# First weight group of a fused GLA/RetNet trunk: tokens loaded on a second queue, larger pieces, ScalarE splits, pinned order

## Chip, cores and metric

The kernel runs on one core of one Trainium2 chip. The metric is the device time of one execution in microseconds (us). Three runs of the kernel before took 1416.07, 1416.16 and 1417.53 us; their median, 1416.16 us, is the time before.

## What is computed

Two layers on 256 tokens of width 2048, each with a residual add, and a final RMSNorm. Layer one is gated linear attention, layer two is retention. Cut to what matters here:

```
h = x
h = h + gla_mixer(rms_norm(h, gla_norm), w_in, w_a1, w_a2, b_a, head_g, w_out)
    proj  = h @ w_in                       # q, k, v, gate
    log_a = log_sigmoid((h @ w_a1) @ w_a2 + b_a) / 16     # low-rank decay, rank 16
    o     = chunked attention with decay; o = rms(o) * head_g
    return (o * silu(gate)) @ w_out
h = h + retention_mixer(rms_norm(h, ret_norm), ...)
return rms_norm(h, final_norm)
```

All data are float32. The kernel keeps float32 accuracy by splitting each operand into two float32r parts: `hi`, the operand rounded by a copy, and `lo`, the operand minus `hi`. A product is then hi·hi + hi·lo + lo·hi.

## The kernel before

All weights lie in 60 groups of 2048 x 512 (16 k-tiles of 128 rows, called kt here). A group is loaded in four `raw` tiles of four k-tiles (1 MB, SyncE's queue, SP). Each raw tile is split in two halves of two k-tiles ("a pair"): ScalarE (ACT) writes `hi` (L151) and VectorE (DVE) writes `lo` (L152). TensorE (PE) then multiplies. Three buffers each of raw, hi and lo let the splits run ahead of TensorE.

The change is in the first group, `gqk0` (q and k of GLA head 0), which `group_w` computes: for each pair `j` = 0..7 and each k-tile, four matmuls of weight-hi with both parts of the tokens (L219, 512 columns) and four of weight-lo with the tokens' hi (L220, 256 columns), into four PSUM tiles. While it runs, the tokens have to be prepared too: `x_t`, the transposed input, comes in tiles `xt0`..`xt3` of four k-tiles (L281), and `make_xhl(kt)` writes the two parts of one k-tile of tokens times the norm's weight `gla_norm` (in `smalls`, L292) to `xhl`: the hi part by a TENSOR_SCALAR (L287) and the lo part by a SCALAR_TENSOR_TENSOR (L288), both on VectorE. In program order `make_xhl` for the k-tiles of pair j+1 is called in `first_group(j)`.

`first_group` also computes the low-rank decay's first product `zps` = x_t · w_a1 (L369, 48 columns of weights, 512 of tokens, one matmul a k-tile). For it `w_a1` is loaded (L309, `wa1_src`) and split by ScalarE (L345) and VectorE (L346) into `wa1`. In program order the two `zps` matmuls of pair j-1 stand behind the gqk matmuls of pair j. A memset of `wa2_src` on GpSimd (POOL, L355), which takes over the buffer of `xt0`, and the loads of `w_a2` (L357) and of `mask_t` (L353, a table first used in the attention scores) follow at j = 6.

The order on each engine isn't the program's: a scheduler of the tile layer orders the instructions by a timeline that it reckons at build time. What is wrapped in `keep` (`tc.keep_in_program_order`) stays in its place in program order; in the kernel before no gqk matmul is. `tc.stamp_issue_order_token(ins, "first")`, new in the change, fixes the order of the stamped instructions among each other. On the chip each engine, and each DMA queue, goes through its list strictly in order, held up only by semaphores.

Before the first weights come, two f32 matmuls on zeros (L272) run on TensorE, and ScalarE's first ACTIVATE (L266), on `lnone`, brings the load of its function table ahead of the first split.

Of the kernel before, what the change touches and what calls it, by code (L numbers as in the profile page):

```python
# [10 lines left out]
F32 = mybir.dt.float32  # L11
# [3 lines left out]
AF = mybir.ActivationFunctionType  # L15
ALU = mybir.AluOpType

P = 128
# [5 lines left out]
SUB = 2  # L24
# [31 lines left out]
def kernel(  # L56
# [17 lines left out]
    nc = tc.nc  # L74
# [17 lines left out]
    mm = nc.tensor.matmul  # L92
    keep = tc.keep_in_program_order
# [12 lines left out]
    def emit_raw(parts=1):  # L106
        c = emitted["raw"]
        if c >= n_groups * raws_per_group:
            return
        t = raw_p.tile([P, CHUNK, GW], F32, tag="raw", name=f"raw{c}")  # L110
        g, j = divmod(c, raws_per_group)
        src = w_all[g, :, j * CHUNK * GW : (j + 1) * CHUNK * GW].rearrange("p (k n) -> p k n", n=GW)
        step = CHUNK // parts
        raws[c] = t
        emitted["raw"] += 1

        def load(k):
            nc.sync.dma_start(t[:, k * step : (k + 1) * step, :], src[:, k * step : (k + 1) * step, :])

        if parts > 1:  # L120
            return load
        load(0)
# [13 lines left out]

    tails = []

    def emit_split(pieces=1):
        i = emitted["sub"]  # L140
        if i >= n_groups * NSUB:
            return
        c, j = divmod(i, per_raw)
        while emitted["raw"] <= min(c + DMA_LOOK, n_groups * raws_per_group - 1):
            emit_raw()
        src = raws[c][:, j * SUB : (j + 1) * SUB, :]
        hi, lo = split_tiles(i)
        step = SUB // pieces
        for k in range(pieces):
            sl = slice(k * step, (k + 1) * step)  # L150
            nc.scalar.activation(hi[:, sl], src[:, sl], AF.Copy)  # L151
            nc.vector.tensor_tensor(lo[:, sl], src[:, sl], hi[:, sl].bitcast(F32), ALU.subtract)  # L152
        splits[i] = (hi, lo)
        if j == per_raw - 1:
            del raws[c]
        emitted["sub"] += 1
# [46 lines left out]
    def group_w(rhs, name, extra=None):  # L203
        ps = [acc_p.tile([P, 2, SEQ], F32, tag="acc", name=f"{name}_ps{c}") for c in range(4)]
        for j in range(NSUB):
            hi, lo = next_weights()
            last = j == NSUB - 1
            order = [(q, c) for q in range(SUB) for c in range(4)]
            if last:
                order = [(q, c) for c in range(4) for q in range(SUB)]  # L210
            for q, c in order:
                kt = j * SUB + q
                wh = hi[:, q, c * P : (c + 1) * P]
                wl = lo[:, q, c * P : (c + 1) * P]
                if kt == NKT - 1:
                    mm(ps[c][:, 0, :], wl, rhs[:, kt, 0, :], start=False, stop=False)
                    mm(ps[c], wh, rhs[:, kt, :, :], start=False, stop=True)
                else:
                    mm(ps[c], wh, rhs[:, kt, :, :], start=kt == 0, stop=False)  # L219
                    mm(ps[c][:, 0, :], wl, rhs[:, kt, 0, :], start=False, stop=False)  # L220
            if extra is not None:
                extra(j)
            advance()
        return ps
# [38 lines left out]

    lnone = const([P, 2], "lnone")
    nc.gpsimd.memset(lnone, 1.0)
    nc.scalar.activation(lnone[:, 1:2], lnone[:, 0:1], AF.Copy)  # L266
    lnone = lnone[:, 0:1]
    warm = sg_p.tile([P, GW], F32, tag="sg", name="warm")
    nc.gpsimd.memset(warm, 0.0)
    warm_ps = mis_p.tile([P, GW], F32, tag="mis", name="warm_ps")  # L270
    for _ in range(2):
        mm(warm_ps, warm[:, 0:P], warm, start=True, stop=True)  # L272

    xts = {}

    def load_xt(c):
        t = t4_p.tile([P, 4, SEQ], F32, tag="t4", name=f"xt{c}")
        xts[c] = t

        def load(lo, hi):  # L280
            nc.sync.dma_start(t[:, lo:hi, :], x_t[:, c * 4 + lo : c * 4 + hi, :])  # L281

        return load

    def make_xhl(kt):
        src, g = xts[kt // 4][:, kt % 4, :], sm[:, S_GN + kt : S_GN + kt + 1]
        nc.vector.tensor_scalar(xhl[:, kt, 0], src, g, None, ALU.mult)  # L287
        nc.vector.scalar_tensor_tensor(  # L288
            xhl[:, kt, 1], src, g, xhl[:, kt, 0].bitcast(F32), ALU.mult, ALU.subtract
        )  # L290

    nc.scalar.dma_start(sm, smalls)  # L292
    x0 = load_xt(0)
    x0(0, 1)
    w0 = emit_raw(4)
    w0(0)
    x0(1, 2)
    w0(1)
    x0(2, 4)
    w0(2)  # L300
    w0(3)
    x1 = load_xt(1)
    x1(0, 2)
    w1 = emit_raw(2)
    w1(0)
    x1(2, 4)
    w1(1)
    wa1_src = t4_p.tile([P, NKT, 16], F32, tag="qk", name="wa1_src", bufs=1)
    nc.sync.dma_start(wa1_src, w_a1)  # L309
    load_xt(2)(0, 4)  # L310
    emit_raw()
    make_xhl(0)
    emit_split(2)
    make_xhl(1)
    wa1 = t4_p.tile([P, NKT, 48], F32R, tag="lc", name="wa1", bufs=1)
    nc.gpsimd.memset(wa1.bitcast(F32), 0.0)

# [25 lines left out]
    def first_group(j):  # L343
        if j == 0:
            nc.scalar.activation(wa1[:, :, 0:16], wa1_src, AF.Copy)  # L345
            nc.vector.tensor_tensor(  # L346
                wa1[:, :, 32:48], wa1_src, wa1[:, :, 0:16].bitcast(F32), ALU.subtract
            )
        if j == 1:
            load_xt(3)(0, 4)  # L350
        if j == 6:
            keep(nc.sync.dma_start(ident, ident_in))
            nc.sync.dma_start(mask_t, mask_in)  # L353
            wr = t4_p.tile([80, 2, GW], F32, tag="t4", name="wa2_src")
            nc.gpsimd.memset(wr, 0.0)  # L355
# [12 lines left out]
        for kt in kts if j else ():  # L368
            mm(zps, wa1[:, kt, :], xhl[:, kt, :, :], start=kt == 0, stop=kt == NKT - 1)  # L369
# [622 lines left out]
```

## Time and profile before

| what | value |
|---|---|
| median of 3 runs | 1416.16 us |
| the profiled execution's own time | 1417.53 us |
| its span in the profile | 1415.8 us |
| TensorE busy | 1403.9 us, 99% of the span |
| VectorE, ScalarE, GpSimd busy | 908.6, 690.4, 46.1 us |
| first gqk matmul, first matmul of the next group (gv) | 4.70, 36.14 us |
| HBM read | 263.49 MB |

The profile lists, for each engine, how long it was busy, and for each idle stretch what ended it (the releaser). In the timeline a row is one or several equal instructions: start, length, engine, line, operation, output<-inputs, shape, count, and in brackets the idle time ahead of it and its releaser. The view by windows gives for a stretch of time the busy time of each engine, then the clock that TensorE was granted (1.00 is full) and the DMA engines' share and rate. Times count from the start of the span. The profiled execution is the slowest of the three; it took 1.7 us more than its span.

### The profile page before, as it was taken

What the parts mean: (1) busy time and instruction counts of PE and PEld (TensorE: products, weight loads), DVE (VectorE), ACT (ScalarE), POOL (GpSimd) and SP (SyncE); (2) the same over time, 40 slices, a digit from 0 to 9 for tenths busy, and PEclk for the clock granted to TensorE, in tenths of its full rate; (3) what the DMA queues carried; (4) which work ended last, traced back from release to release, by engine and by line L of the source; (5) the groups of instructions that cost most, each with busy time, mean ns of one, the idle gap of its engine ahead of it and who ended that gap; (6) DMA issues with size and microseconds to landing.
All of it is one profiled execution on the core that took longest, in us unless ns stands there. A gap on an engine that the chain in (4) does not pass through costs nothing.

```text
span 1415.8 us, 17504 instructions
## 1 busy us (share of the span) xinstructions
PE 1403.9 (99%) x6800; PEld 1180.0 (83%) x6800; DVE 908.6 (64%) x1430; ACT 690.4 (49%) x889; POOL 46.1 (3%) x98
## 2 busy tenths in 40 slices
PE   8999999999999999999999999999999999999997
PEld 6888888888888888888888888888888888888887
DVE  6685796545845774665766666665556666666664
ACT  3665655534555655554444444444334444444453
POOL 0001020000010020000000000000000000000000
PEclk9999999999999999999999999999999999999999
DMA  8654555555555555555555555555555555555662
GB/s 287 240 177 149 192 180 175 183 204 180 177 179 178 188 189 179 178 178 183 190 194 192 194 189 198 179 199 181 203 182 184 196 184 199 182 203 176 209 212 94
DMA packets 40499, 266.72 MB, mean 188 GB/s; under 512 B 4880, under 2 KB 5392, under 8 KB 9696
## 3 DMA queue, kind: packets, MB, share of 16 engines
q1 hardware_dynamic: 37536, 257.57, 53.9%
q0 software_dynamic: 2160, 6.95, 1.5%
q8 instruction: 53, 0.87, 0.2%
q10 hardware_dynamic: 720, 1.09, 0.2%
q14 instruction: 30, 0.25, 0.0%
HBM read 263.49 MB, written 2.10 MB: 188 GB/s over the span
## 4 chain that ended last, share of the span: by engine, by line
PE 99%; DMA 0%; SPq 0%; DVE 0%; ACT 0%; issue 0%
PE rqk_ps L219 8%; PE gv_ps L184 4%; PE gg_ps L185 4%; PE rv_ps L184 4%; PE gv_ps L185 4%; PE gv_ps L186 4%; PE rv_ps L185 4%; PE rv_ps L186 4%; PE gg_ps L186 4%; PE gg_ps L184 4%; PE rg_ps L184 4%; PE rg_ps L185 4%; PE rg_ps L186 4%; PE rqk_ps L220 4%; PE gqk_ps L219 4%; PE gb_ps L184 2%
## 5 line engine op out<-in xcount | busy, mean ns | idle before, releaser
L152 DVE TENSOR_TENSOR lo<-raw,hi 128x1024 fp32r<-128x1024 f32 (+1 forms) x473 | 576.6, 1222 | 420.7 <-ACT hi L151 419.9
L151 ACT ACTIVATE hi<-raw 128x1024 fp32r<-128x1024 f32 (+1 forms) x473 | 499.5, 1057 | 614.4 <-PE rg_ps L186 104.6
L219 PE MATMUL rqk_ps<-xhl,hi 128*128 128x512 f32 x480 | 166.9, 398 | 0.0
L220 PE MATMUL rqk_ps<-xhl,lo 128*128 128x256 f32 x480 | 126.4, 280 | 0.0
L219 PEld LDWEIGHTS rqk_ps<-xhl,hi 128*128 128x128 f32 x480 | 88.8, 188 | 17.5
L185 PE MATMUL gg_ps<-lo,xhl 128*128 128x512 f32 x256 | 100.5, 393 | 0.0
L185 PE MATMUL gv_ps<-lo,xhl 128*128 128x512 f32 x256 | 100.4, 392 | 0.0
L185 PE MATMUL rv_ps<-lo,xhl 128*128 128x512 f32 x256 | 100.4, 392 | 0.0
L186 PE MATMUL gv_ps<-hi,xhl 128*128 128x512 f32 x256 | 100.3, 392 | 0.0
L186 PE MATMUL gg_ps<-hi,xhl 128*128 128x512 f32 x256 | 100.0, 391 | 0.0
L186 PE MATMUL rv_ps<-hi,xhl 128*128 128x512 f32 x256 | 99.7, 389 | 0.0
L185 PE MATMUL rg_ps<-lo,xhl 128*128 128x512 f32 x256 | 99.6, 389 | 0.0
L186 PE MATMUL rg_ps<-hi,xhl 128*128 128x512 f32 x256 | 99.6, 389 | 0.0
L184 PE MATMUL gv_ps<-hi,xhl 128*128 128x512 f32 x256 | 93.1, 391 | 0.0
L184 PE MATMUL rv_ps<-hi,xhl 128*128 128x512 f32 x256 | 92.1, 390 | 0.0
L220 PEld LDWEIGHTS rqk_ps<-xhl,lo 128*128 128x128 f32 x480 | 89.1, 189 | 3.4
L184 PE MATMUL rg_ps<-hi,xhl 128*128 128x512 f32 x256 | 91.8, 389 | 0.0
L184 PE MATMUL gg_ps<-hi,xhl 128*128 128x512 f32 x256 | 91.8, 391 | 0.0
L219 PE MATMUL gqk_ps<-xhl,hi 128*128 128x512 f32 x240 | 81.2, 406 | 1.6 <-ACT hi L151 1.6
L220 PE MATMUL gqk_ps<-xhl,lo 128*128 128x256 f32 x240 | 57.9, 283 | 0.5 <-DVE lo L152 0.5
L186 PEld LDWEIGHTS rv_ps<-hi,xhl 128*128 128x128 f32 x256 | 48.1, 188 | 10.0
L186 PEld LDWEIGHTS rg_ps<-hi,xhl 128*128 128x128 f32 x256 | 48.0, 188 | 10.0
(265 smaller groups left out, 2381.8 us busy)
## 6 DMA issues: line engine op xcount, KB each, us to landing
raw<-in_w_all SPq DMA_DIRECT2D x238, 1024.0 KB, 4.9
resid<-in_x_n SPq DMA_DIRECT2D x2, 1024.0 KB, 8.0
gg<-in_gn_g POOLq DMA_DIRECT2D x8, 256.0 KB, 3.8
gb<-in_gn_b POOLq DMA_DIRECT2D x8, 256.0 KB, 4.5
dm<-in_dmat POOLq DMA_DIRECT2D x8, 192.0 KB, 2.6
raw<-in_w_all SPq DMA_DIRECT2D x4, 256.0 KB, 5.0
raw<-in_w_all SPq DMA_DIRECT2D x2, 512.0 KB, 7.4
xt<-in_x_t SPq DMA_DIRECT2D x2, 512.0 KB, 8.5
```

What stands on the lines that cost most here:

```text
L151: nc.scalar.activation(hi[:, sl], src[:, sl], AF.Copy)
L152: nc.vector.tensor_tensor(lo[:, sl], src[:, sl], hi[:, sl].bitcast(F32), ALU.subtract)
L184: mm(ps, xh, hi[:, q, :], start=kt == 0, stop=False)
L185: mm(ps, xh, lo[:, q, :], start=False, stop=False)
L186: mm(ps, xl, hi[:, q, :], start=False, stop=kt == NKT - 1)
L219: mm(ps[c], wh, rhs[:, kt, :, :], start=kt == 0, stop=False)
L220: mm(ps[c][:, 0, :], wl, rhs[:, kt, 0, :], start=False, stop=False)
```

## The change

Seven edits, all in the start of the kernel:

- The tokens of k-tiles 0 and 1 are loaded by ScalarE's DMA queue, the first of them ahead of `smalls`; ScalarE's table load follows these three issues.
- Larger pieces: the second half of `raw0` comes in one DMA in place of two, `xt1` in one in place of two; `w_a1` is loaded behind `xt2`, no longer ahead of it.
- The hi part of the tokens of k-tiles 1 to 7 is made by ScalarE in place of VectorE.
- One of the two warming matmuls is cut to 128 columns.
- The first splits and the first four k-tiles of tokens are stamped to stay in program order, and `make_xhl(1)` is called between the two pieces of the first split.
- For pairs 0 to 2 of the first group all gqk matmuls are kept in program order, four hi and then four lo for each k-tile.
- The mask's load goes from SyncE's to GpSimd's queue, later in program order.

```diff
-        def load(k):
-            nc.sync.dma_start(t[:, k * step : (k + 1) * step, :], src[:, k * step : (k + 1) * step, :])
+        def load(k, n=1):
+            sl = slice(k * step, (k + n) * step)
+            nc.sync.dma_start(t[:, sl, :], src[:, sl, :])
...
-            nc.scalar.activation(hi[:, sl], src[:, sl], AF.Copy)
-            nc.vector.tensor_tensor(lo[:, sl], src[:, sl], hi[:, sl].bitcast(F32), ALU.subtract)
+            a = nc.scalar.activation(hi[:, sl], src[:, sl], AF.Copy)
+            b = nc.vector.tensor_tensor(lo[:, sl], src[:, sl], hi[:, sl].bitcast(F32), ALU.subtract)
+            if i == 0:
+                first(a, b)
+                if k == 0:
+                    between()
...
+            if j < 3 and extra is not None:
+                for q in range(SUB):
+                    kt = j * SUB + q
+                    for c in range(4):
+                        keep(mm(ps[c], hi[:, q, c * P : (c + 1) * P], rhs[:, kt, :, :], start=kt == 0, stop=False))
+                    for c in range(4):
+                        keep(mm(ps[c][:, 0, :], lo[:, q, c * P : (c + 1) * P], rhs[:, kt, 0, :], start=False, stop=False))
+                order = []
...
-    for _ in range(2):
-        mm(warm_ps, warm[:, 0:P], warm, start=True, stop=True)
+    mm(warm_ps, warm[:, 0:P], warm, start=True, stop=True)
+    mm(warm_ps[:, 0:P], warm[:, 0:P], warm[:, 0:P], start=True, stop=True)
...
+    def first(*ins):
+        for x in ins:
+            tc.stamp_issue_order_token(x.ins, "first")
...
-        nc.vector.tensor_scalar(xhl[:, kt, 0], src, g, None, ALU.mult)
-        nc.vector.scalar_tensor_tensor(
+        if 0 < kt < 8:
+            a = nc.scalar.activation(xhl[:, kt, 0], src, AF.Copy, scale=g)
+        else:
+            a = nc.vector.tensor_scalar(xhl[:, kt, 0], src, g, None, ALU.mult)
+        b = nc.vector.scalar_tensor_tensor(
...
+    x0 = load_xt(0)
+    x0(0, 1, nc.scalar)
     nc.scalar.dma_start(sm, smalls)
-    x0 = load_xt(0)
-    x0(0, 1)
+    x0(1, 2, nc.scalar)
+    nc.scalar.activation(lnone2, lnone, AF.Copy)
     w0 = emit_raw(4)
     w0(0)
-    x0(1, 2)
     w0(1)
     x0(2, 4)
-    w0(2)
-    w0(3)
-    x1 = load_xt(1)
-    x1(0, 2)
+    w0(2, 2)
+    load_xt(1)(0, 4)
     w1 = emit_raw(2)
     w1(0)
-    x1(2, 4)
     w1(1)
     wa1_src = t4_p.tile([P, NKT, 16], F32, tag="qk", name="wa1_src", bufs=1)
+    load_xt(2)(0, 4)
     nc.sync.dma_start(wa1_src, w_a1)
-    load_xt(2)(0, 4)
     emit_raw()
     make_xhl(0)
-    emit_split(2)
-    make_xhl(1)
+    emit_split(2, lambda: make_xhl(1))
...
-            nc.sync.dma_start(mask_t, mask_in)
...
+        nc.gpsimd.dma_start(mask_t, mask_in)
```

How this moves the lists of instructions, at the places that the prediction speaks of. TensorE before, at the first use of `wa1`: `hi3` and `lo3` are the parts of pair 3, `hi4` of pair 4, `gqk0_ps` are the group's four PSUM tiles; a row's bracket names the semaphore it waits for.

```order
L219 MATMUL gqk0_ps2_162<-xhl_100,hi3_196 128x512
L220 MATMUL gqk0_ps2_162<-xhl_100,lo3_197 128x256
L219 MATMUL gqk0_ps3_163<-xhl_100,hi3_196 128x512
L220 MATMUL gqk0_ps3_163<-xhl_100,lo3_197 128x256
L369 MATMUL zps_159<-xhl_100,wa1_151 48x512 [waits DVE_49]
L369 MATMUL zps_159<-xhl_100,wa1_151 48x512 x7
L369 MATMUL zps_159<-xhl_100,wa1_151 48x512 [waits DVE_49] x4
L219 MATMUL gqk0_ps0_160<-xhl_100,hi4_226 128x512 [waits Activation_49]
```

TensorE in the changed kernel, at the first use of `wa1` (its lines have higher numbers: L152 and L153 are the splits L151 and L152, L220 and L222 the gqk matmuls, L306 and L307 the tokens' L287 and L288, L386 is `zps`).

```order
L222 MATMUL gqk0_ps2_160<-xhl_100,lo1_163 128x256
L222 MATMUL gqk0_ps3_161<-xhl_100,lo1_163 128x256
L386 MATMUL zps_157<-xhl_100,wa1_149 48x512 [waits DVE_49]
L386 MATMUL zps_157<-xhl_100,wa1_149 48x512
L220 MATMUL gqk0_ps0_158<-xhl_100,hi2_168 128x512
L220 MATMUL gqk0_ps1_159<-xhl_100,hi2_168 128x512
```

Before, the scheduler put the first twelve `zps` matmuls behind pair 3; now the first two stand behind pair 1, the kept matmuls of pair 2 come after them, and two more follow each later pair.

VectorE in the changed kernel, from the split of pair 1 to the one of pair 4.

```order
L153 TENSOR_TENSOR lo1_163<-raw0_123,hi1_162 128x1024 [waits DMAHW6_49,Activation_49]
L307 SCALAR_TENSOR_TENSOR xhl_100<-xt1_128,smalls_97,xhl_100 128x256 [waits DMAHW7_49,Activation_49]
L307 SCALAR_TENSOR_TENSOR xhl_100<-xt1_128,smalls_97,xhl_100 128x256 [waits Activation_49] x3
L153 TENSOR_TENSOR lo2_169<-raw1_130,hi2_168 128x1024 [waits DMAHW0_49,Activation_49]
L153 TENSOR_TENSOR lo3_195<-raw1_130,hi3_194 128x1024 [waits DMAHW1_49,PE_49,Activation_49]
L306 TENSOR_SCALAR xhl_100<-xt2_134,smalls_97 128x256 [waits DMAHW2_49]
L306 TENSOR_SCALAR xhl_100<-xt2_134,smalls_97 128x256 x3
L364 TENSOR_TENSOR wa1_149<-wa1_src_133,wa1_149 128x16x16 [waits DMAHW3_49,Activation_49]
L307 SCALAR_TENSOR_TENSOR xhl_100<-xt2_134,smalls_97,xhl_100 128x256 [waits DVE_49] x4
```

The lo part of `wa1` (L364), for which the first `zps` matmul waits, stands behind `lo3` and four TENSOR_SCALAR of `xt2`; before it stood behind `lo3` too, ahead of the tokens of `xt2`.

SyncE's queue in the changed kernel, from its first DMA.

```order
L119 DMA raw0_123<-in_w_all 128x512 x2
L293 DMA xt0_118<-in_x_t 128x512
L119 DMA raw0_123<-in_w_all 128x1024
L293 DMA xt1_128<-in_x_t 128x1024
L119 DMA raw1_130<-in_w_all 128x1024 [waits DMAHW0_49]
L119 DMA raw1_130<-in_w_all 128x1024 [waits DMAHW1_49]
L293 DMA xt2_134<-in_x_t 128x1024 [waits DMAHW2_49]
L329 DMA wa1_src_133<-in_w_a1 128x256 [waits DMAHW3_49]
L119 DMA raw2_137<-in_w_all 128x2048 [waits DMAHW4_49]
```

Before, this list began with the tokens of k-tile 0, the tokens of k-tile 1 stood between the first two pieces of `raw0`, and `wa1_src` stood between `raw1` and `xt2`. GpSimd's list has one row more: the mask's DMA, directly behind the memset of `wa2_src`. Behind the first GLA head the lists agree row for row.

More of the change, by code (lines that the diff above doesn't have):

```diff
@@ L137, with emit_split @@
     tails = []
-    def emit_split(pieces=1):
+    def emit_split(pieces=1, between=None):
         i = emitted["sub"]
@@ L265 @@
     nc.gpsimd.memset(lnone, 1.0)
-    nc.scalar.activation(lnone[:, 1:2], lnone[:, 0:1], AF.Copy)
-    lnone = lnone[:, 0:1]
+    lnone, lnone2 = lnone[:, 0:1], lnone[:, 1:2]
     warm = sg_p.tile([P, GW], F32, tag="sg", name="warm")
@@ L278, in load_xt, with load @@
         xts[c] = t
-        def load(lo, hi):
-            nc.sync.dma_start(t[:, lo:hi, :], x_t[:, c * 4 + lo : c * 4 + hi, :])
-        return load
+        def load(lo, hi, eng=nc.sync):
+            eng.dma_start(t[:, lo:hi, :], x_t[:, c * 4 + lo : c * 4 + hi, :])
+        return load
+    def first(*ins):
+        for x in ins:
+            tc.stamp_issue_order_token(x.ins, "first")
     def make_xhl(kt):
         src, g = xts[kt // 4][:, kt % 4, :], sm[:, S_GN + kt : S_GN + kt + 1]
-        nc.vector.tensor_scalar(xhl[:, kt, 0], src, g, None, ALU.mult)
-        nc.vector.scalar_tensor_tensor(
+        if 0 < kt < 8:
[3 more added lines that the diff above has]
+        b = nc.vector.scalar_tensor_tensor(
             xhl[:, kt, 1], src, g, xhl[:, kt, 0].bitcast(F32), ALU.mult, ALU.subtract
         )
+        if kt < 4:
+            first(a, b)
+    x0 = load_xt(0)
+    x0(0, 1, nc.scalar)
     nc.scalar.dma_start(sm, smalls)
-    x0 = load_xt(0)
-    x0(0, 1)
+    x0(1, 2, nc.scalar)
+    nc.scalar.activation(lnone2, lnone, AF.Copy)
     w0 = emit_raw(4)
     w0(0)
-    x0(1, 2)
     w0(1)
     x0(2, 4)
-    w0(2)
-    w0(3)
-    x1 = load_xt(1)
-    x1(0, 2)
+    w0(2, 2)
+    load_xt(1)(0, 4)
     w1 = emit_raw(2)
     w1(0)
-    x1(2, 4)
     w1(1)
     wa1_src = t4_p.tile([P, NKT, 16], F32, tag="qk", name="wa1_src", bufs=1)
+    load_xt(2)(0, 4)
     nc.sync.dma_start(wa1_src, w_a1)
-    load_xt(2)(0, 4)
     emit_raw()
     make_xhl(0)
-    emit_split(2)
-    make_xhl(1)
+    emit_split(2, lambda: make_xhl(1))
     wa1 = t4_p.tile([P, NKT, 48], F32R, tag="lc", name="wa1", bufs=1)
```

## Prediction

> **What bounds the kernel now.** I read the page's engine table first, then the list of waits of TensorE alone, then TensorE's timeline up to the first matmul of the second group.
>
> ```profile
> span 1415.8 us, 17504 instructions
> PE 1403.9 (99%) x6800; PEld 1180.0 (83%) x6800; DVE 908.6 (64%) x1430; ACT 690.4 (49%) x889; POOL 46.1 (3%) x98
> ...
> PE warm_ps L272 <- POOL warm L269: 1.8, 1, 1.8
> PE gqk_ps L219 <- ACT hi L151: 1.6, 2, 1.2
> PE gqk_ps L220 <- DVE lo L152: 0.5, 1, 0.5
> ```
>
> TensorE is busy for 99% of the span, and the whole list of its waits has three lines, all in the first 13 us. So the change can take nothing off the rest of the kernel; it can shift the moment at which the first group is done, and everything behind moves by as much. The first group in TensorE's timeline:
>
> ```profile
> 4.70 1.96 PE L219 MATMUL gqk_ps<-xhl,hi 128*128 128x512 f32 x4
> ...
> 7.50 1.19 PE L219 MATMUL gqk_ps<-xhl,hi 128*128 128x512 f32 x4 [0.36 <-ACT hi L151]
> ...
> 10.35 1.19 PE L219 MATMUL gqk_ps<-xhl,hi 128*128 128x512 f32 x4 [1.20 <-ACT hi L151]
> 12.09 0.83 PE L220 MATMUL gqk_ps<-xhl,lo 128*128 128x256 f32 x4 [0.55 <-DVE lo L152]
> ...
> 15.28 1.43 PE L219 MATMUL gqk_ps<-xhl,hi 128*128 128x512 f32 x4
> ...
> 21.23 2.94 PE L369 MATMUL zps<-xhl,wa 128*48 128x512 f32 x12
> 24.02 1.08 PE L219 MATMUL gqk_ps<-xhl,hi 128*128 128x512 f32 x4
> ...
> 26.82 1.09 PE L219 MATMUL gqk_ps<-xhl,hi 128*128 128x512 f32 x4
> ...
> 36.14 0.47 PE L184 MATMUL gv_ps<-hi,xhl 128*128 128x512 f32 x1
> ```
>
> K-tile 0 starts at 4.70, k-tile 1 at 7.50, pair 1 (k-tiles 2 and 3) at 10.35, pair 2 at 15.28, and the next group at 36.14. From 12.09 on TensorE never waits. A pair takes 2.80 us at full clock (24.02 to 26.82). The clock is the second thing to see, in stretches chosen to fit its changes:
>
> ```profile
> core 0: us, PE busy (x) PEld busy (x) DVE busy (x) ACT busy (x) POOL busy (x), PEclk, DMA share, GB/s
> 2.00:9.00 7.00, 6.63 (x20) 3.88 (x20) 3.71 (x9) 1.92 (x4) 0.94 (x5) 1.00 0.87 264
> 10.00:13.00 3.00, 2.10 (x9) 1.59 (x10) 2.72 (x6) 1.36 (x2) 0.49 (x1) 0.93 1.03 411
> 9.18:12.59 3.41, 1.69 (x8) 1.18 (x9) 2.61 (x6) 2.11 (x2) 0.95 (x1) 1.00 1.02 403
> 12.59:16.00 3.41, 3.41 (x13) 2.93 (x12) 3.41 (x7) 1.36 (x2) 0.00 (x0) 0.50 1.04 430
> 16.00:19.40 3.40, 3.40 (x20) 2.88 (x20) 3.40 (x11) 1.89 (x2) 0.00 (x0) 1.00 1.10 370
> ```
>
> In the 3.41 us from 9.18 TensorE was busy for 1.69, half the time; in the next 3.41 us it was granted half the clock, and, busy throughout, full clock after that. The price was 3.41 x 0.5 = 1.7 us of work. So the idle times of 1.20 and 0.55 us cost themselves and 1.7 us more.
>
> Everything from pair 2 on needs 36.14 - 15.28 = 20.86 us, of which 0.36 is the half clock's (0.72 us, 15.28 to 16.00, at half speed): **20.50 us of work**, six pairs and all sixteen `zps`. The change leaves this work as it is. So the result follows from two numbers: when TensorE is let through to pair 2 and its first `zps`, against 15.28, and how much half clock comes after, against 0.36.
>
> **The change, part by part.** The part that decides is not named in the change's title. The first two `zps` now stand behind pair 1 and ahead of the kept matmuls of pair 2. They wait for the lo part of `wa1`, and TensorE goes in order: pairs 2 to 7, all of the 20.50 us, queue behind that wait. Before, the same `zps` stood behind pair 3 and waited for nothing (21.23 has no bracket). On VectorE the lo part of `wa1` stands behind `lo3` and four TENSOR_SCALAR of `xt2`; `lo3` needs `hi3`, and `hi3` the second half of `raw1`. So TensorE now waits for data of pair 3 before it may start pair 2. The chain's durations:
>
> ```profile
> 9.24 1.06 ACT L151 ACTIVATE hi<-raw 128x1024 fp32r<-128x1024 f32 x1 [1.80 <-DMA raw<-in_w_all]
> ...
> 13.51 1.06 ACT L151 ACTIVATE hi<-raw 128x1024 fp32r<-128x1024 f32 x1 [0.97 <-DMA raw<-in_w_all]
> 14.47 0.40 ACT L345 ACTIVATE wa<-wa_src 128x256 fp32r<-128x256 f32 x1
> ...
> 15.20 1.21 DVE L152 TENSOR_TENSOR lo<-raw,hi 128x1024 fp32r<-128x1024 f32 x1
> 16.33 0.41 DVE L346 TENSOR_TENSOR wa<-wa_src,wa 128x256 fp32r<-128x256 f32 x1
> 16.67 1.13 DVE L287 TENSOR_SCALAR xhl<-xt,smalls 128x256 fp32r<-128x256 f32 x4
> 17.72 0.47 DVE L288 SCALAR_TENSOR_TENSOR xhl<-xt,smalls,xhl 128x256 fp32r<-128x256 f32 x1
> ```
>
> `hi3` takes 1.06 us, `lo3` 1.13 (15.20 to 16.33, the next start), the four TENSOR_SCALAR 1.05 (16.67 to 17.72), the lo part of `wa1` 0.41; with 0.1 for the hand-overs, an estimate, 3.75 us from the arrival of `raw1`'s second half.
>
> That arrival was 13.51 before. Three edits move it. The order of the bytes ahead is the same, but 0.786 MB of them (`raw0`'s second half, half of `xt1`) come in rows of 4 KB in place of 2 KB. The stretch with the small pieces, 2 to 9 us, ran at 264 GB/s, the one with mostly 4 KB rows at 411: 0.786 MB take 1.91 in place of 2.98 us, a gain of 1.07. I take all of it, since nothing else in the two rows differs as clearly; the other end is no gain. The tokens on ScalarE's queue let the first weights be issued at 0.74 in place of 1.19:
>
> ```profile
> 0.74 0.39 SPq L281 DMA_DIRECT2D xt<-in_x_t  x1
> 1.19 0.42 SPq L118 DMA_DIRECT2D raw<-in_w_all  x1
> ...
> 10.27 0.33 SPq L353 DMA_DIRECT2D mask<-in_mask  x1
> ...
> 9.54 0.95 POOL L355 MEMSET wa_src<- 80x1024 f32 x1 [6.60 <-DVE xhl L288]
> ```
>
> That is between 0 and 0.45 us for the bytes behind, and I take 0.22. The mask, issued at 10.27 behind everything of the first pairs before, now follows GpSimd's memset, which began at 9.54 when the tokens of k-tile 3 were done and would begin about 1 us earlier; its 0.26 MB (0.64 us at 411 GB/s) run on another queue beside `raw1` and may delay it by 0 to 0.64; I take 0.32. The mask itself isn't waited for before the attention scores. So `raw1`'s second half arrives at 13.51 - 1.07 - 0.22 + 0.32 = 12.54, and the first `zps` starts at **16.29**. `w_a1` and `xt2`, next in the queue, carry 0.66 MB, 1.6 us: there by 14.1, and ScalarE's 0.40 is done by 14.6, before VectorE is through `lo3` (14.8). Bounds: all 3.18 MB ahead at 411 GB/s from 2.0 us give 9.7, and `zps` at 13.5; no gain at all and the mask's full price give 14.15, and `zps` at 17.9. I stay near the row of before.
>
> TensorE is through with pair 1 well ahead of that. `raw0`'s second half arrived at 9.24; less 0.71 (0.524 MB at the better rate) and 0.22 that is 8.31; `hi1` 1.06 and `lo1` 1.21 end at 10.6, and the last twelve matmuls of the pair, two thirds of 2.80 us, at 12.5. It then **idles for 3.8 us**, as long as the stretch after which the clock was halved, which had been idle for 1.7 us only. So I count another stretch at half clock, 1.7 us, all of it now on the 20.50 us. Released half-way it is 0.85; if the stretch in which work resumes doesn't count and a second follows, 3.4.
>
> The sum: 16.29 - 15.28 = +1.01 for the wait, 1.70 - 0.36 = +1.34 for the clock: **+2.35 us**. The other edits come out at nothing. The three removed waits (0.36, 1.20, 0.55) and the 1.35 us of half clock ahead of 15.28 all lie before the new wait, which swallows any gain. The seven TENSOR_SCALAR taken from VectorE (1.13 a four) and put on ScalarE (0.40 each, by the row of the same shape) lie there too, since ScalarE was waiting for loads in both rows above. The shorter warming ends sooner, but k-tile 0 waits for its split anyway; at worst the clock rises one stretch later, which is again ahead of the wait. Were the wait hidden, that cover would be gone, and the removed idle times would count in full.
>
> A rule of the Trainium skill speaks against the gain in loading: the page "DMA: Bandwidth & Descriptors", section "🎯 Rules for kernel authors", says that spreading DMAs over several engines brings no bandwidth, only the sequencers' issue time. By it the 0.22 may stand, and the second queue gives nothing else; the sum would not change by more.
>
> **From the span to the time.** The profiled execution took 1417.53 us for its span of 1415.8; with the change it would take 1419.88. It was the slowest of the three; on their median, 1416.16, the forecast is **1418.5 us**. The wait between 15.6 and 17.0 and a price of 1.3 to 2.3 us for the clock give 1417.4 to 1419.8.
>
> **Rivals.**
>
> - *The loads come no sooner.* For it: the 264 GB/s may be those of a queue that is just starting, not of short rows. Arrival 13.51 - 0.22 + 0.64 = 13.93, `zps` at 17.68, +2.40 + 1.34 = +3.74: 1419.9; with two stretches of half clock 1421.6.
> - *The clock holds through the stall.* Against it: the row 9.18:12.59, where 1.7 us of idle time sufficed. For it: one case only. Then +1.01 - 0.36 = +0.65: 1416.8. The page "TensorE: Matmul & The Clock Gate" of the Trainium skill, section "🎯 Why this matters for your kernels", allows gaps up to about 3 us and takes the clock back after a whole idle window; by that rule the gaps of before, 1.20 and 0.55, would have been free, which the trace contradicts.
> - *Faster: the loads run at full pace from the first byte.* Arrival 9.7, `zps` at 13.45: -1.83 + 1.34 = -0.49, 1415.7; with the clock held too, 1414.0. It turns at `raw1`'s second half arriving before 10.2. Against it: k-tiles 0 and 1 still come in the 1 and 2 KB rows of the 264 GB/s stretch.
> - *The change doesn't do what it says*: TensorE doesn't stop at the first `zps`, since VectorE has `wa1` by 12.5. For that `raw1` would have to be there at 8.8, before the earliest bound; I give it nothing of its own.
>
> **How the numbers follow.** Forecast 0.58, later loads 0.22, clock held 0.14, full pace 0.06. A measurement of this kernel can tell about 0.2%, 2.8 us, from no change: slower means over 1419.0. A third of the forecast's share and all of the later loads lie there: 0.41. Faster, under 1413.3, is left with the last rival's far end, 0.02; the rest, 0.57, is within. The range leaves out the full pace, a little of the held clock, and the upper half of the later loads: 1416.2 to 1420.8.
>
> **What would show it.** In the changed trace a row of `zps`, x2 or x4, behind pair 1, with an idle time of 2.5 to 5 us released by VectorE's `wa`, starting at 15.5 to 17; the hi split of `raw1`'s second half about 3.7 us ahead of it; a stretch at 0.50 that covers `zps` and pair 2; the first gv matmul at 38.5 in place of 36.14; and no other wait of TensorE behind it. Wrong would be: a gv matmul before 36, `zps` without a bracket, or new waits in the second group.

## The result and the profile after

The changed kernel takes 1419.12 us (median of 22 runs, 1417.70 to 1420.92), the kernel before 1417.22 us (22 runs beside them, 1415.86 to 1418.76). The ratio is 1.0014, 95% interval [1.0008, 1.0021]: 1.9 us slower, and less than the 2.8 us named as the bound. The profiled execution of the changed kernel took 1419.77 us for a span of 1418.0, against 1417.53 and 1415.8 before: 2.24 us more, where the sum said 2.35. The times of the kernel before fall in two groups some 1.4 us apart, and its median, taken again beside each set of the runs below, was 1416.11 to 1416.38 there, so times of different sets compare to about 1 us only.

The list of TensorE's waits in the changed kernel, whole (us in total, times, longest):

```profile
PE zps L386 <- DVE wa L364: 2.6, 1, 2.6
PE warm_ps L283 <- POOL warm L281: 1.8, 1, 1.8
PE gqk_ps L220 <- DVE xhl L307: 1.7, 1, 1.7
```

The three small waits at the first weights (1.2, 0.5 and 0.4 us) are gone. Two others stand in their place: one at the first `zps`, one at the first matmul of the group. TensorE's timeline of the changed kernel:

```profile
1.81 2.08 PE L283 MATMUL warm_ps<-warm 128*128 128x512 f32 x2 [1.81 <-POOL warm L281]
3.68 0.64 PE L284 MATMUL warm_ps<-warm 128*128 128x128 f32 x2
6.03 2.04 PE L220 MATMUL gqk_ps<-xhl,hi 128*128 128x512 f32 x4 [1.72 <-DVE xhl L307]
...
8.72 1.35 PE L220 MATMUL gqk_ps<-xhl,hi 128*128 128x512 f32 x4
...
10.38 1.08 PE L220 MATMUL gqk_ps<-xhl,hi 128*128 128x512 f32 x4
...
12.70 0.63 PE L222 MATMUL gqk_ps<-xhl,lo 128*128 128x256 f32 x4
15.98 1.02 PE L386 MATMUL zps<-xhl,wa 128*48 128x512 f32 x2 [2.65 <-DVE wa L364]
16.80 1.91 PE L220 MATMUL gqk_ps<-xhl,hi 128*128 128x512 f32 x4
...
20.84 0.61 PE L386 MATMUL zps<-xhl,wa 128*48 128x512 f32 x2
...
38.05 0.40 PE L189 MATMUL gv_ps<-hi,xhl 128*128 128x512 f32 x1
```

K-tile 0 starts at 6.03, 1.3 us later than before. Pairs 0 and 1 then run without a gap, and TensorE stops for 2.65 us at the first `zps`. The next group starts at 38.05, 1.91 us later than before; nothing waits behind it. From there to the end of the span it takes 1379.95 us, against 1379.66 before. So 1.91 of the 2.2 us between the spans arose ahead of 38 us; the other 0.29 us lie behind, and where is not known. The windows of the changed kernel, cut where the clock changed:

```profile
2.00:9.00 7.00, 5.28 (x13) 3.60 (x14) 3.20 (x7) 4.46 (x8) 0.94 (x5) 1.00 0.96 334
12.68:16.09 3.41, 0.77 (x6) 0.53 (x5) 3.41 (x8) 0.69 (x2) 0.00 (x0) 1.00 1.00 419
16.09:19.50 3.41, 3.41 (x11) 2.70 (x12) 2.92 (x7) 1.06 (x1) 0.00 (x0) 0.50 1.05 314
19.50:22.90 3.40, 3.40 (x20) 2.88 (x19) 2.90 (x8) 1.08 (x2) 0.00 (x0) 1.00 1.02 366
```

The clock column (1.00, 1.00, 0.50, 1.00) doesn't tell everything: in the first row it says 1.00 too, although four gqk matmuls of 512 columns took 2.04 us there (6.03) and 1.08 at 10.38. Up to the first full clock, here near 9.3 us, the lengths of TensorE's rows tell it.

The stretch with the stall has 0.77 us of TensorE work, and the one behind it runs at half clock. VectorE has 3.41 of 3.41 us in the stretch in which TensorE stands. Its timeline shows with what:

```profile
9.46 1.22 DVE L153 TENSOR_TENSOR lo<-raw,hi 128x1024 fp32r<-128x1024 f32 x1 [0.26 <-ACT hi L152]
10.61 1.67 DVE L307 SCALAR_TENSOR_TENSOR xhl<-xt,smalls,xhl 128x256 fp32r<-128x256 f32 x4
12.19 2.35 DVE L153 TENSOR_TENSOR lo<-raw,hi 128x1024 fp32r<-128x1024 f32 x2
14.46 1.13 DVE L306 TENSOR_SCALAR xhl<-xt,smalls 128x256 fp32r<-128x256 f32 x4
15.51 0.41 DVE L364 TENSOR_TENSOR wa<-wa_src,wa 128x256 fp32r<-128x256 f32 x1
```

From 9.46 to 15.9 there is no gap: `lo1`, four tokens, `lo2` and `lo3`, four tokens of `xt2`, and only then the lo part of `wa1`.

### The profile page after: what moved, and what is told of

Its sections match the earlier page's. It is cut to its first block, busy times and chain, and to the rows that moved or that the text cites. A ratio compares the mean times of both kernels' runs of the same rounds, so it can differ in the third digit from the quotient of the medians.

```text
span 1418.0 us, 17505 instructions
## 1 busy us (share of the span) xinstructions
PE 1403.7 (99%) x6800; PEld 1181.0 (83%) x6800; DVE 907.0 (64%) x1423; ACT 693.1 (49%) x896; POOL 46.5 (3%) x99
## 3 DMA queue, kind: packets, MB, share of 16 engines
q10 hardware_dynamic: 1008, 1.35, 0.3%
## 4 chain that ended last, share of the span: by engine, by line
PE 98%; DVE 0%; ACT 0%; DMA 0%; issue 0%; ACTq 0%
PE rqk_ps L232 8%; PE gv_ps L189 4%; PE gg_ps L189 4%; PE rv_ps L189 4%; PE gv_ps L190 4%; PE rv_ps L190 4%; PE gg_ps L190 4%; PE gv_ps L191 4%; PE gg_ps L191 4%; PE rv_ps L191 4%; PE rg_ps L189 4%; PE rg_ps L190 4%; PE rg_ps L191 4%; PE rqk_ps L233 4%; PE gqk_ps L232 4%; PE gb_ps L189 2%
## 5 line engine op out<-in xcount | busy, mean ns | idle before, releaser
L153 DVE TENSOR_TENSOR lo<-raw,hi 128x1024 fp32r<-128x1024 f32 (+1 forms) x473 | 576.6, 1222 | 425.0 <-ACT hi L152 424.4
L152 ACT ACTIVATE hi<-raw 128x1024 fp32r<-128x1024 f32 (+1 forms) x473 | 499.5, 1057 | 608.3 <-PE rg_ps L191 104.6
L232 PE MATMUL gqk_ps<-xhl,hi 128*128 128x512 f32 x216 | 73.3, 397 | 0.0
L190 PEld LDWEIGHTS rg_ps<-lo,xhl 128*128 128x128 f32 x256 | 48.1, 188 | 10.0
```

Source lines behind the costliest of these rows:

```text
L152: a = nc.scalar.activation(hi[:, sl], src[:, sl], AF.Copy)
L153: b = nc.vector.tensor_tensor(lo[:, sl], src[:, sl], hi[:, sl].bitcast(F32), ALU.subtract)
L190: mm(ps, xh, lo[:, q, :], start=False, stop=False)
```

## The theories and the experiments

**Theory:** pinning pairs 0 to 2 puts TensorE in front of `wa1` before pair 2. That wait and one stretch of half clock behind it are the whole loss, and what the other edits gain or lose ahead of the wait is covered by it. **Rival A:** the loss comes from the late start (6.03 against 4.70). **Rival B:** the arrival of the loads alone decides when the wait ends, and VectorE's list does not matter.

### 1. The first zps behind pair 3

```diff
+        if j <= 3:
+            kts = range(0, 6) if j == 3 else ()
```

> The changed kernel with one edit: the first six zps matmuls are emitted behind pair 3 instead of two each behind pairs 1 to 3. Theory (TensorE's wait at the first zps is the whole loss): pair 1 ends at 13.2 as before, pair 2 follows at once since lo2 is done by 13.3, no half clock after the first 10 us, the next group starts near 13.2 + 20.5 = 33.7 in place of 38.05, so about 4.3 us less than the changed kernel and 2.4 us less than the kernel before: near 1414.8. Rival (the later or slower loads cost the time, the zps only show it): pair 2 or 3 waits instead, for its hi or lo part, and the time stays within 1 us of the changed kernel, near 1419.

Measured: 1416.31 us, ratio to before 0.9998 [0.9989, 1.0007]; the span is 1414.8. TensorE's only waits are the warming's and this one:

```profile
6.14 2.05 PE L220 MATMUL gqk_ps<-xhl,hi 128*128 128x512 f32 x4 [1.82 <-DVE xhl L307]
...
10.55 1.05 PE L222 MATMUL gqk_ps<-xhl,lo 128*128 128x256 f32 x4
11.40 1.26 PE L220 MATMUL gqk_ps<-xhl,hi 128*128 128x512 f32 x4
```

The `zps` matmuls wait for nothing, the next group starts at 34.88 in place of 38.05, and the median is 2.8 us lower. So the loss is that wait, and rival A falls as its cause, since the late start (6.14) is still there. But the kernel is no faster than before, though it has none of the three old waits, and the expected 1414.8 was missed: four lo matmuls take 1.05 us until 11.4, against 0.64 at full clock. Uncovered, the late start and half clock until about 11.8 eat the gain.

### 2. The stall filled with work

```diff
+        if j == 1:
+            for _ in range(3):
+                keep(mm(warm_ps, warm[:, 0:P], warm, start=True, stop=True))
```

> The changed kernel with three more warming matmuls (f32, 512 columns, on zeros) between pair 1 and the first zps: they take some 0.85 us each at full clock and fill the idle 2.65 us. Theory (the half clock behind the stall is a cost of its own, 1.7 us, set by idleness): zps starts at 15.9 to 16.1 as in the changed kernel, the clock stays at 1.00, the next group starts near 36.4 in place of 38.05, time about 1.7 us under the changed kernel, 1417.4. Rival (the clock falls for another reason, or the fill delays zps by its own 2.6 us): half clock still seen, or zps past 16.5; time 1419 or more.

Measured: 1418.62 us, 1.0015 [1.0006, 1.0024]. TensorE's timeline:

```profile
14.92 2.74 PE L387 MATMUL warm_ps<-warm 128*128 128x512 f32 x6
17.10 1.02 PE L389 MATMUL zps<-xhl,wa 128*48 128x512 f32 x2
```

The granted clock behind the wait is 1.00 here (next group 20.9 us after `zps`, against 22.1 in the changed kernel), and no run has the 0.997 that 11 of the changed kernel's 22 runs have. The time did not follow: `zps` started at 17.10, about 1.3 us after `wa1` would have let it (done at 15.72), since the filling ran too long, as the rival said. The clock's share is shown; as a remedy this is none.

### 3. The load of w_a1 ahead of xt2 again

```diff
-    load_xt(2)(0, 4)
     nc.sync.dma_start(wa1_src, w_a1)
+    load_xt(2)(0, 4)
```

> The changed kernel with w_a1 loaded ahead of xt2 again. On VectorE the lo part of wa1 then stands ahead of the four TENSOR_SCALAR of xt2. Theory (VectorE's list behind lo3 sets the first zps): lo3 still ends near 14.5, zps starts 1.05 us sooner, near 14.9, the idle time is 1.6 us; with the same half clock about 1.0 us under the changed kernel, 1418.1, and 0.6 us over the kernel before. Rival (the arrival of w_a1 sets it): w_a1 arrives 1.2 us sooner, at 12.1, and zps starts right behind its split, at 13.5 or before, 2.4 us under the changed kernel.

Measured: 1416.97 us, 1.0003 [0.9994, 1.0012]; span 1415.1, next group at 35.17. VectorE, then TensorE:

```profile
11.82 2.36 DVE L153 TENSOR_TENSOR lo<-raw,hi 128x1024 fp32r<-128x1024 f32 x2
14.09 0.42 DVE L364 TENSOR_TENSOR wa<-wa_src,wa 128x256 fp32r<-128x256 f32 x1
14.43 1.14 DVE L306 TENSOR_SCALAR xhl<-xt,smalls 128x256 fp32r<-128x256 f32 x4
```

```profile
13.66 0.63 PE L222 MATMUL gqk_ps<-xhl,lo 128*128 128x256 f32 x4
14.57 0.66 PE L386 MATMUL zps<-xhl,wa 128*48 128x512 f32 x2 [0.28 <-DVE wa L364]
```

With `w_a1` ahead of `xt2` in the queue its lo part stands ahead of the four TENSOR_SCALAR of `xt2` on VectorE, `zps` comes 1.4 us sooner, and the clock holds in the profile. Of the 1.4 us, the order on VectorE gives the 1.05 that four TENSOR_SCALAR take; the rest is that `lo2` began 0.37 us sooner in this execution. Two swapped lines take most of the loss away, with the pinned order still there. So in the changed kernel the new place of this load makes the pinned order dearer; that the pinned order loses without it as well, run 4 shows.

### 4. The kernel before with pairs 0 to 2 pinned

```diff
+            if j < 3 and extra is not None:
+                for q in range(SUB):
+                    kt = j * SUB + q
+                    for c in range(4):
+                        keep(mm(ps[c], hi[:, q, c * P : (c + 1) * P], rhs[:, kt, :, :], start=kt == 0, stop=False))
+                    for c in range(4):
+                        keep(mm(ps[c][:, 0, :], lo[:, q, c * P : (c + 1) * P], rhs[:, kt, 0, :], start=False, stop=False))
+                order = []
```

> The kernel before with one part of the change alone: the gqk matmuls of pairs 0 to 2 kept in program order, all else as before. Theory (the keep, which puts the first zps ahead of pair 2, carries the whole loss): TensorE waits at the first zps for VectorE's part of wa1, which was done at 16.7 in the kernel before, so zps starts near 16.8 after 1.5 us idle, and the next group at 16.8 + 20.5 = 37.3 without, or 38.9 with another stretch of half clock: 1.2 to 2.8 us over the kernel before. Rival (the loss comes from the loads' new order and queues): no change from before, within 0.5 us.

Measured: 1420.22 us, 1.0019 [1.0011, 1.0028]. VectorE's lo part of `wa1` and TensorE's `zps`:

```profile
15.43 1.21 DVE L152 TENSOR_TENSOR lo<-raw,hi 128x1024 fp32r<-128x1024 f32 x1
16.56 0.41 DVE L354 TENSOR_TENSOR wa<-wa_src,wa 128x256 fp32r<-128x256 f32 x1
```

```profile
17.03 0.66 PE L377 MATMUL zps<-xhl,wa 128*48 128x512 f32 x2 [1.03 <-DVE wa L354]
```

One edit of seven carries a loss of the same kind as all seven together, and by the medians a larger one: 4.0 us over the kernel before in its set, more than the 1.2 to 2.8 expected. The profiled execution, 1418.80, is one of three shorter runs of the 11; its next group starts at 37.49, 1.35 us later than before. The stall shows as 1.03 us only, since the old waits ahead of pair 1 (here 2.27 us, and a stretch of half clock from 12.32) already made TensorE late. An idle time is no measure of a wait's cost; the start of what stands behind it is.

### 5. The tokens' hi part on VectorE again

```diff
-        if 0 < kt < 8:
+        if False:
```

> The changed kernel with the hi part of the tokens of k-tiles 1 to 7 made by VectorE again. Theory (VectorE's list from the split of pair 1 to wa1, busy without a gap from 9.5 to 15.9 in the changed kernel, sets the first zps): four more TENSOR_SCALAR in that list, 1.1 to 1.3 us, so zps near 17.2 and the next group near 39.3, time 1.2 us over the changed kernel, 1420.3. Rival (the arrival of raw1's second half sets it): zps within 0.3 us of 15.98 and no change in time.

Measured: 1421.34 us (5 runs), 1.0038 [1.0023, 1.0052]. VectorE, then TensorE:

```profile
15.07 1.22 DVE L153 TENSOR_TENSOR lo<-raw,hi 128x1024 fp32r<-128x1024 f32 x1
16.21 1.13 DVE L306 TENSOR_SCALAR xhl<-xt,smalls 128x256 fp32r<-128x256 f32 x4
17.26 0.41 DVE L364 TENSOR_TENSOR wa<-wa_src,wa 128x256 fp32r<-128x256 f32 x1
```

```profile
17.73 0.43 PE L386 MATMUL zps<-xhl,wa 128*48 128x512 f32 x1 [3.24 <-DVE wa L364]
```

ScalarE's `hi3` began at 11.58 here, so the data were there as early as in the changed kernel; `lo3` began only at 15.07, since VectorE had seven TENSOR_SCALAR more ahead of it. `zps` and the next group (39.77) are 1.7 us later and the median about 2.2 higher. VectorE's list sets the wait as much as the loads do: rival B falls. ScalarE's hi part is worth some 2 us in the changed kernel.

### 6 to 8. What is hidden ahead of the wait, with zps behind pair 3

Tokens back on SyncE's queue (6), both long warming matmuls back (7), and both (8), each on top of the edit of 1:

```diff
-    x0(0, 1, nc.scalar)
     nc.scalar.dma_start(sm, smalls)
-    x0(1, 2, nc.scalar)
+    x0(0, 1)
...
     w0(0)
+    x0(1, 2)
```

```diff
-    mm(warm_ps, warm[:, 0:P], warm, start=True, stop=True)
-    mm(warm_ps[:, 0:P], warm[:, 0:P], warm[:, 0:P], start=True, stop=True)
+    for _ in range(2):
+        mm(warm_ps, warm[:, 0:P], warm, start=True, stop=True)
```

> The kernel with zps behind pair 3 and the tokens of k-tiles 0 and 1 on SyncE's queue again, ahead of their weights, smalls first on ScalarE's. Theory (the second queue makes tokens, smalls and weights share the engines from the first byte, so that smalls arrives at 5.0 in place of 3.3 and the first matmul starts at 6.1 in place of 4.7): first matmul near 4.75, clock up one stretch sooner in most runs, pair 2 near 12.5, the next group near 33.4 in place of 34.9, time 1.4 us less: 1414.9. Rival (the late start is due to the weights' earlier issue alone, or is hidden by the later loads): first matmul at 5.5 or later, or an unchanged time near 1416.3 because pairs 1 and 2 wait for their splits instead.

> The kernel with zps behind pair 3 and both warming matmuls in full length again, the tokens still on ScalarE's queue. Theory (the short warming leaves TensorE idle from 4.3 to 6.1 and the clock at half until 11.8): full clock from 5.8 to 9.2 on, k-tiles 0 and 1 in 2.9 us in place of 4.1 to 5.2, pair 1 bound by its split near 9.3, the next group near 33.5, time 1.4 us less than with the short warming: 1414.9. Rival (warming doesn't matter, the first matmuls raise the clock themselves in the same stretch): full clock at the same time after the first gqk matmul as with the short warming, time unchanged, 1416.3.

> Both together: zps behind pair 3, tokens on SyncE's queue, full warming. First matmul near 4.75 at once behind the warming, full clock from 5.8 on. Theory: TensorE then waits for the splits of k-tile 1 and pair 1, some 1.5 to 2 us in all, pair 2 near 12.5, the next group near 33.3, time 1414.7 in runs without another stretch of half clock and 1416.1 in runs with one. Rival (the idle times of k-tile 1 and pair 1 always halve the clock again): all runs near 1416.

Measured: 1416.38 us, 1.0001 [0.9992, 1.001] for 6; 1416.01, 0.9997 [0.9988, 1.0006] for 7; 1415.86, 1.0 [0.9991, 1.001] for 8. The times do not tell them apart, and none comes to the expected 1414.7 to 1414.9; the profiled executions do differ. In 6 the first gqk matmul starts at 4.86, but TensorE waits for splits of `raw0`, 0.54 us at k-tile 0 and 0.67 at pair 1, since the second half of `raw0` comes later, and the next group starts at 34.04 (in 8 at 33.70):

```profile
PE gqk_ps L220 <- ACT hi L152: 1.2, 2, 0.7
```

In 7 TensorE is on full clock from its first gqk matmul, with the next group at 32.79, the earliest of all profiled executions:

```profile
1.81 3.78 PE L284 MATMUL warm_ps<-warm 128*128 128x512 f32 x4 [1.81 <-POOL warm L281]
6.28 1.15 PE L220 MATMUL gqk_ps<-xhl,hi 128*128 128x512 f32 x4 [0.68 <-DVE xhl L307]
```

That execution took 1414.51 us, but only 3 of the 11 runs of 7 were under 1415; the others lay between 1415.65 and 1416.65. So the short warming cost up to 2 us of clock in 1, in some runs, and the second queue exchanged waits for the splits of `raw0` for a late start.

### 9 and 10. A version that should beat both

On top of 7, `smalls` first on ScalarE's queue (9), and on top of 9 a third long warming matmul (10).

```diff
+    nc.scalar.dma_start(sm, smalls)
     x0(0, 1, nc.scalar)
-    nc.scalar.dma_start(sm, smalls)
```

```diff
-    for _ in range(2):
+    for _ in range(3):
         mm(warm_ps, warm[:, 0:P], warm, start=True, stop=True)
```

> The changed kernel with the first six zps behind pair 3 and both long warming matmuls, and now the norm's weights (smalls) first on ScalarE's queue, ahead of the two k-tiles of tokens. My theory: the first token part on VectorE was held by smalls alone (landed 4.9; 3.3 where they were first), so k-tile 0 starts at about 5.3 in place of 6.28, without the idle time behind the warming, the clock is up from about 6 in every run, gv starts at 32.2 to 32.8 and the time is 1414.0 to 1415.0, faster than before by 1 to 2 us. Rival: a tile of tokens is late in its turn (k-tile 0 or 1 lands 0.5 later), TensorE waits there instead, gv stays at 32.8 and the time at 1416.0 as with smalls second.

> As the kernel with smalls first, with a third long warming matmul, about 0.9 us of full-clock work that fills the gap between the warming and k-tile 0. My theory, that what separates the two clusters of times is whether an idle gap near 5.6 to 6.3 falls into a clock stretch: TensorE has no idle time over 0.3 us from 1.8 on, all runs lie in one cluster of 1414.0 to 1415.2, with a granted clock of 0.999. Rival: the third matmul ends behind the tokens' arrival and delays k-tile 0 by up to 0.9; then gv lies at 33.0 to 33.6 and the time at 1415.0 to 1415.8, no better than with two.

Measured: 1415.61 us, 0.9991 [0.9982, 1.0] for 9; 1415.12, 0.9989 [0.998, 0.9997] for 10. The time of 9 lies above the expected 1414.0 to 1415.0, and my theory that `smalls` alone held the first token falls. VectorE's first operation in 9:

```profile
5.07 0.35 DVE L306 TENSOR_SCALAR xhl<-xt,smalls 128x256 fp32r<-128x256 f32 x1 [5.07 <-DMA xt<-in_x_t]
```

It now waits for the token in place of `smalls` (5.01 in the changed kernel): swapping the two did not change when this operation starts. What 9's median owes to chance stays open. 10 has no idle time in TensorE at all behind 1.81 us:

```profile
1.81 5.49 PE L284 MATMUL warm_ps<-warm 128*128 128x512 f32 x6 [1.81 <-POOL warm L281]
6.32 2.08 PE L220 MATMUL gqk_ps<-xhl,hi 128*128 128x512 f32 x4
```

All its 11 runs lie between 1414.73 and 1415.81, in one cluster, though four of them above the expected 1415.2. It is the only version that is faster than before beyond its interval, by 1.3 us. Its profiled execution has the next group at 33.36, behind 32.79 in 7: the rival's delay is there too. That steadiness outweighs it is read from the times of two different sets.

### 11 and 12. The same two edits undone with the wait in place

The diffs of 7 and of 6, without the edit of 1: `zps` stands ahead of pair 2.

> The changed kernel with both long warming matmuls and nothing else; zps still stands ahead of pair 2. With zps behind pair 3 the long warming brought gv from 34.88 to 32.79, by 2.1 us. My theory (edits ahead of the wait are covered by it): pair 1 ends 1 to 2 us sooner, the idle time ahead of zps grows by as much (to about 4), zps still starts at 15.8 to 16.2 by VectorE's lo part of wa1, one stretch of half clock follows, gv at 37.8 to 38.3, time 1418.5 to 1419.5 as the changed kernel. Rival: the longer warming moves the clock's stretches, so that the idle time fills a whole one or none is lost behind zps: gv at 36.3 (clock held) or 39.8 (two stretches).

> The changed kernel with the two k-tiles of tokens on SyncE's queue again; zps still stands ahead of pair 2. My theory: k-tile 0 starts at 4.8 in place of 6.0, which the wait covers; the loads of weights are issued 0.4 us later, so raw1's second half lands 0 to 0.5 later, but VectorE, which was the later of the two, starts its chain sooner too: zps at 15.8 to 16.5, gv at 37.9 to 38.6, time 1418.5 to 1419.7, no difference from the changed kernel beyond the interval. Rival: the second queue was what brought raw1 0.76 us sooner than forecast; then zps at 16.7 to 17.0 and the time 0.7 to 1.0 longer, 1419.8 to 1420.4.

Measured: 1419.31 us, 1.0021 [1.0012, 1.003] for 11: long warming gives nothing while the wait stands, as the theory says. (Its profiled execution, at 1417.83 the shortest of the 11, kept the clock behind `zps`, with the next group at 36.16 as the rival said.) 12 took 1420.77 us (8 runs), 1.0028 [1.0018, 1.0038], longer than the changed kernel by about 1.6 and than 11, in the same set, by 1.5: here the rival is right, and by more than it asked. The windows, VectorE, TensorE and the landing (512 KB, 8.9 us after its issue at 4.5) of `raw1`'s second half in 12:

```profile
2.00:9.00 7.00, 5.95 (x20) 3.82 (x20) 2.78 (x6) 3.05 (x7) 0.94 (x5) 1.00 0.94 281
```

```profile
16.90 0.42 DVE L364 TENSOR_TENSOR wa<-wa_src,wa 128x256 fp32r<-128x256 f32 x1
```

```profile
17.38 0.67 PE L386 MATMUL zps<-xhl,wa 128*48 128x512 f32 x2 [1.68 <-DVE wa L364]
```

```profile
raw<-in_w_all SPq DMA_DIRECT2D x1, 512.0 KB, 8.9
```

With the tokens on SyncE's queue the half tile lands at 13.4 in place of 11.8, and `zps` starts 1.4 us later. The next group starts at 37.90 all the same, 0.15 sooner than in the changed kernel, because the clock held behind `zps` in this execution, the shortest of the eight (1419.38). The edit's gain for the loads behind it was on the path after all. Its size varies: 6 and 8 have the same order of loads as 12, and there the half tile, issued at 4.5 as well, took 8.3 and 8.0 us and landed at 12.8 and 12.5. Their windows, 6 and then 8:

```profile
2.00:9.00 7.00, 6.46 (x17) 4.47 (x18) 3.43 (x7) 3.25 (x7) 1.01 (x6) 1.00 0.93 288
2.00:9.00 7.00, 6.88 (x20) 4.10 (x20) 3.50 (x7) 3.48 (x8) 1.28 (x6) 1.00 0.96 300
```

## Why the prediction was right, and which terms were off

The profiled executions, in us:

| version | `zps` | next group | between | clock behind `zps` |
|---|---|---|---|---|
| changed kernel | 15.98 | 38.05 | 22.07 | one stretch at half |
| 5, hi on VectorE | 17.73 | 39.77 | 22.04 | one stretch at half |
| 3, `w_a1` first | 14.57 | 35.17 | 20.60 | full |
| 4, before + pinned | 17.03 | 37.49 | 20.46 | full |
| 11, long warming | 15.72 | 36.16 | 20.44 | full |
| 12, tokens on SyncE | 17.38 | 37.90 | 20.52 | full |

- **The step that decides was right.** `zps` waits for VectorE's lo part of `wa1` ahead of pair 2: forecast 16.29 with 3.8 us idle, measured 15.98 with 2.65 (pair 1 ended later than forecast, behind the late start). Runs 1, 3 and 4 show it as the cause by taking it away, by shortening it and by adding it alone.
- **The work behind it was right.** 20.50 us was forecast; the four rows at full clock have 20.44 to 20.60. The clock's price of one stretch was right too: 22.07 - 20.50 = 1.57 against 1.70. It is not the same in every run: the profiled execution of 11, with 1.77 us of idle time ahead of `zps`, kept its clock and took 1417.83, while the median of its runs was 1419.31. The changed kernel's own 22 runs fall in two groups as well, 10 up to 1418.67 at a granted clock of 0.998 or 0.999 and 12 from 1419.09, all but one at 0.997. So keeping the clock, the rival that the prediction gave 0.14, likely happened in nearly half of the runs. The kernel before has as many short runs, so the difference stays near 2 us from short to short as from long to long; the two profiled executions are both long ones, and of what the difference of two short ones is made no trace shows.
- **The second queue's share of the arrival was mis-sized.** Larger pieces were given 1.07 us, the moved mask 0.32 against it, the second queue 0.22. Runs 12, 6 and 8 have the larger pieces and the moved mask, but not the second queue: `raw1`'s second half lands at 13.4, 12.8 and 12.5, against 13.4 before (issued at 5.66, plus 7.7). So pieces and mask gave 0 to 0.9 us, where 0.75 was forecast, and the second queue, which brings the landing to 11.8, another 0.7 to 1.6. That the 264 GB/s came from short rows is neither shown nor refuted: with the larger pieces alone the three executions have 281 to 300. Part of the queue's gain is issue time: SyncE issues `raw0`'s second half at 2.12 in place of 3.07 in run 12, since two DMAs of 0.45 us no longer stand ahead of it; I counted the first weight's 0.45 only, and half of that. Whether the rate rose beyond that isn't settled. The rule of the Trainium skill that was weighed there, from the page "DMA: Bandwidth & Descriptors", section "🎯 Rules for kernel authors", allows the issue time and denies more bandwidth. Against run 12 some 0.7 us of the gain is left beyond the 0.95 of issue time, against run 8 nothing. What the mask costs by itself was not tried.
- **VectorE's backlog was missing.** The sum added 3.75 us to the arrival; it was 4.2 (11.8 to 15.98). With the earlier arrival `lo3` could have begun at 13.0 (`hi2` and `hi3` are done at 12.96), and began about 0.4 later, since VectorE was still at `lo2`. Run 5 shows the larger mistake: in the prediction ScalarE's hi part is one of the edits that "come out at nothing", because it lies ahead of the wait. It does lie ahead, but on VectorE, whose list ends in the very operation that is waited for; without this edit the wait ends 1.75 us later.
- **Warming at nothing was right, for the second reason given** (a later clock is still ahead of the wait; k-tile 0 itself waited for its tokens, not for its split): run 11 with both long matmuls is the changed kernel again, while in run 7, without the wait, the same edit brought the next group from 34.88 to 32.79 in the profile. The tokens' late start was covered as well, but was not forecast at all: 6.03 in place of 4.70, from `smalls` at 4.9 in place of 3.3.
- **The base was low.** Profiled execution against profiled execution the sum (+2.35) met the measurement (+2.24). The forecast then stood on the median of three runs, 1416.16. The 22 runs of before fall in two clusters 1.4 us apart, and their median is 1417.22; the measured difference of the medians is +1.90. The two deviations, +1.06 and -0.45, leave the time 0.6 above the forecast. In part that is luck: the forecast hits the middle of neither group of the changed kernel's runs (1417.99 and 1419.49), and of the +2.24 only 1.91 is the shift of the next group that the sum was about; the 0.29 behind it was in no term. The wait came out at +0.70 for +1.01, the clock at +1.21 for +1.34.

Where the expected gain of the loads went: the three old waits (2.1 us) and their half clock lie ahead of the new wait, which swallows their removal. The prediction held that they would count in full if the wait were hidden. Run 1 hides it, and they don't: the next group is 1.26 us sooner in the profile and the time unchanged, since the late start and the late clock give most of it back. With these mended too (10) the gain is 1.3 us.

## What to carry to other kernels

Pinning one stream of instructions also pins whatever the program emits between its parts: read the engine's list for the first instruction that jumped ahead, and the producer's list for all that stands before what it waits for. A gain ahead of an in-order wait is worth nothing unless it also moves the producer; a gain on the producer's list counts in full, even on an engine that looks idle on average. Compare time behind the wait (from its end to the next group) apart from the time to it: a clock that drops then shows as a longer rest, and an early arrival as an earlier end.

## What the runs showed of the hardware

**The clock.** In the traces read here it changes only at the ends of stretches of 3.41 us: in the changed kernel it falls at 16.09 and rises at 19.50, and its first rise, near 9.3 by the lengths of the rows, is two such stretches ahead of the fall. The stretch behind one with 0.77 (above), 1.33 (12) or 0.72 us (5) of TensorE work was at half clock; one behind 1.64 us (11) was not, yet before the change one behind 1.69 was. The windows of 12, 5 and 11:

```profile
8.65:12.06 3.41, 1.33 (x6) 0.73 (x5) 2.22 (x4) 2.87 (x6) 1.57 (x2) 1.00 1.01 401
```

```profile
15.04:18.45 3.41, 0.72 (x3) 0.54 (x4) 3.41 (x10) 1.06 (x1) 0.00 (x0) 1.00 1.04 431
```

```profile
13.48:16.89 3.41, 1.64 (x10) 1.18 (x9) 3.41 (x10) 0.74 (x1) 0.00 (x0) 1.00 1.00 413
```

Near half a stretch of work either can happen, so busy time alone does not decide; what does is open. Where the stretches lie differs from run to run, and a run loses one (1.7 us of work) or not. That is the likely origin of the clusters: of 33 runs of before, 18 had a granted clock of 0.998 or 0.999 and 1415.65 to 1416.36 us, and 15 had 0.997 and 1417.17 to 1418.85.

**A second queue at the start.** With it the first 9 us (from 2 us on) ran at 325 to 349 GB/s in nine profiled executions, without it, at the same pieces, at 281, 288 and 300 in three; how much of that is earlier issue is not separated. The small loads came later: `smalls`, 36.5 KB, lands at 4.9 behind one tile of tokens and at 3.3 alone on its queue. Put first again (9), it landed at 4.1 and the tokens at 5.07. In the profiled execution of 9, the longest of its 11 runs, the second tile of tokens came only at 9.24, 3 us later than in 10, and TensorE waited 2.68 us; why is open.
